# PEER gates of all 128 tokens of the first tile by indirect DMAs; norm scales by a product that also transposes

## The chip, the cores and the metric

One core of one Trainium2 chip runs the program. The metric is device time in microseconds (us), the median of several runs; lower is better. PE is TensorE, DVE VectorE, ACT ScalarE, POOL GpSimd, SP the engine that issues the ordinary DMAs.

## The reference, cut to what matters

256 tokens of width 1024 go through two blocks in float32. Block 1: a mixer (GLA and sparse attention), cross attention to 256 memory tokens, a PEER layer, a final norm. Block 2: a mixer (HGRN and Hyena), a PEER layer, a final norm. Every sublayer starts with an RMS norm.

```python
def rms_norm(x, g):
    y = x * lax.rsqrt(jnp.mean(x * x, axis=-1, keepdims=True) + EPS)
    return y * g

def peer(xb, ...):                     # 8 heads, 16 of 128 x 128 experts each
    ...
    g = jax.nn.softmax(top_s, axis=-1)           # 8 x 16 gates per token
    act = jax.nn.gelu(einsum('td,thkd->thk', xb, down[experts])) * g
    return einsum('thk,thkd->td', act, up[experts])
```

## The kernel before

**PEER, densely.** The kernel doesn't gather experts. `down` multiplies all 16384 experts with all 256 tokens, 128 experts `j` at a time, applies gelu and keeps the result in `Ha` (j below 64) and `Hb`, as [expert row i, j, token]. Most of its entries have gate 0. `up` then multiplies them, each times its gate, with the up table. Both stream 512 KB of weights per `j`: a DMA into `wf` (4 buffers), a cast to `wh` on ACT, a subtraction to `wl` on DVE, then three products per operand pair on PE (`mm3`: float32 as a high and a low part). A load is issued by SP in the order of the code and waits for a free `wf`.

**The gates** reach the 128 x 128 grid in two ways. For tokens 0 to 95 (`NS` = 96) `routing` computes addresses `at`, and `scatter` adds the gates with 128 indirect DMAs (L289, one per head and rank, one element per token) into two zeroed DRAM tensors, `gates1e` and `gates1o`, even and odd heads; each head's DMAs wait for those of the head before it in the same tensor. SP writes the zeros (`grids`, one piece behind each second load). `gates` reads them back, 4 `j` at a time, behind the waits for the scatter, and `halves` multiplies. For tokens 96 to 255, `gate` multiplies one-hot matrices on PE: per group of four tokens four float32 products (L1048), then one multiply on DVE. `_interleave` puts these groups between the pieces of `down`.

**Norms.** `norm_rows` sums squares of the two token tiles (t = 0, 1), takes the power -1/2 on POOL (`rstd`), and writes the scaled rows `xn` (L407 on DVE, L408 on ACT). `to_cols` transposes `xn` on PE, 8 chunks per tile (L424); `split` writes each chunk times the gain as a high part `xch` (L434, ACT) and a low part `xcl` (L437, DVE), which the next products need. There are five such norms (block 1's first, memory, cross attention, and one ahead of each PEER); `between` makes the final norm of block 1 and the first norm of block 2 in one, with rows `xn` too (L1442).

The last two pieces of `up` go together: all four accumulators `acc[t][n]` get both pieces before the next one starts, so that the first is complete while the others still run. Tile's scheduler sets the order on each engine, with waits by semaphores.

Of the kernel before, what the change touches and what calls it, by code (L numbers as in the profile page):

```python
# [28 lines left out]
NS = 96  # L29
# [184 lines left out]
class _Kernel:  # L214
    def __init__(self, tc, ctx, A):
# [11 lines left out]
        self.los = []  # L227
# [30 lines left out]
    def grids(self, name):  # L258


        G = [self.dr.tile([P * P * NS, 1], F32, name=name + y) for y in "eo"]
        v = [y.rearrange("(p x) o -> p (x o)", p=P) for y in G]
        n = P * NS // 12

        def blanks():
            for x in range(24):
                d = self.nc.sync.dma_start(v[x % 2][:, x // 2 * n:x // 2 * n + n].rearrange("p (a t) -> p a t", t=T),
                                           self.zero[:, None, :].to_broadcast([P, n // T, T])).ins
# [47 lines left out]
    def stream(self, src, n=1024, pool_lo=False):  # L316
# [3 lines left out]
        with self.tc.high_priority(offset=1):  # L320
# [9 lines left out]
            if not pool_lo:  # L330
                self.los.append(lo)
            if self.ahead == 3:
# [56 lines left out]
    def square(self, x, ss, dve=False):  # L389
# [4 lines left out]
        else:  # L394
            self.nc.scalar.activation(scr, x, AF.Square, accum_out=ss)

    def norm_rows(self, h, xn, urgent):

        nc = self.nc
        hv, xv = (y.rearrange("p t (a d) -> p t a d", a=2) for y in (h, xn))  # L400
# [9 lines left out]
        return xn  # L410
# [6 lines left out]
    def to_cols(self, src, dst, chunks, gain=None, c0=0):  # L417
# [26 lines left out]
    def norm_cols(self, h, gi, dst, pool, xn=None, urgent=False):  # L444
        xn = pool.tile([P, 2, D], F32, name="xn", tag="xn", bufs=1) if xn is None else xn
        self.norm_rows(h, xn, urgent)
        dst = dst or self.cols("xc")
        self.to_cols(xn, dst, range(8), lambda c: self.gains[:, gi * 8 + c:gi * 8 + c + 1])
        return dst
# [3 lines left out]
    def setup(self):  # L453
# [8 lines left out]
        self.zero = self.pc.tile([P, T], F32, name="zero")  # L462
# [107 lines left out]
    def block1_mix(self, mkT, mc, hm, pf):  # L570
        nc, A, tc = self.nc, self.A, self.tc
        with ExitStack() as st:
            pool = lambda name, bufs=1: st.enter_context(tc.tile_pool(name=name, bufs=bufs))
            p, pn = pool("b1"), pool("nsa")
            with tc.tile_pool(name="b1n", bufs=1) as px:
                x = self.norm_cols(self.h, 0, None, px)
# [4 lines left out]
            with tc.tile_pool(name="gla", bufs=1) as pg, tc.tile_pool(name="glaw", bufs=2) as pw:  # L581
                with tc.tile_pool(name="cmp", bufs=1) as pc:
# [3 lines left out]
                    self.norm_cols(hm, 2, mc, None, hm)  # L586
# [289 lines left out]
    def cross(self, mkT, mv, mem_k, mem_v):  # L876
        nc, A, tc = self.nc, self.A, self.tc
        with tc.tile_pool(name="xa", bufs=2) as pw, tc.tile_pool(name="xa1", bufs=1) as p:
            x = self.norm_cols(self.h, 1, None, pw, urgent=True)
# [46 lines left out]
    def routing(self, pool, qT, sk, split_tiles, res, keep, G):  # L926
# [4 lines left out]
        for i in range(2):  # L931
# [73 lines left out]
            if i == 0:  # L1005
# [9 lines left out]
            s = slice(i * P, i * P + P)  # L1015

            for w in range(2):
                nc.vector.tensor_copy(ji[:, 1 - w, s], b[:, w, :, None].to_broadcast([P, P, 2]))
            nc.vector.tensor_copy(gf[:, s], b[:, 2])
            yield 1  # L1020

    def gate(self, H, res, oh, at):
# [7 lines left out]
        def hot(t0):  # L1030
            ts = slice(t0, t0 + N)
# [8 lines left out]
        for t0 in range(T - N, NS - 1, -N):  # L1040
            (e, a), more = nxt, iter(hot(t0 - N)) if t0 > NS else iter((None, None))
            for t4 in (4, 0):
# [3 lines left out]
                for x in range(4):  # L1046
                    nc.scalar.mul(c[:, x], e[:, t4 + x], gf[:, t0 + t4 + x:t0 + t4 + x + 1])  # L1047
# [39 lines left out]
    def up(self, w, H, G, pool, acc, first):  # L1087
# [11 lines left out]
        for js in [(j,) for j in range(P - 2)] + [(P - 2, P - 1)]:  # L1099
# [18 lines left out]
    def peer(self, x, wq, nq, skname, dn, up, gain, G):  # L1118
        nc, A, tc = self.nc, self.A, self.tc
        with ExitStack() as st:  # L1120
# [3 lines left out]
            pa = e(tc.tile_pool(name="pact", bufs=2))  # L1124
            ha = e(tc.tile_pool(name="pha", bufs=1))
            res = [pi.tile([P, 2, T, 2], BF, name="ji"), pi.tile([P, T], F32, name="g2")]
# [14 lines left out]
            _interleave(self.down(A[dn], range(64, P - 2), x, H, pa, at), self.gate(H, res, oh, at), 0.7)  # L1141
# [278 lines left out]
    def between(self, h, acc, g, y, xn):  # L1420
# [3 lines left out]
        hv, yv, xv = (u.rearrange("p t (a d) -> p t a d", a=2) for u in (h, y, xn))  # L1424
        r1 = []
        for t in range(2):
            sh, sy = [self.small.tile([P, 2], F32, name="ss" + n, tag="ss" + n) for n in "hy"]
# [8 lines left out]
            nc.vector.tensor_scalar(sh[:, 0:1], sh[:, 0:1], 1.0 / D, EPS, op0=ALU.mult, op1=ALU.add)  # L1436
            nc.vector.tensor_scalar(sh[:, 1:2], sh[:, 0:1], EPS, None, op0=ALU.mult)
            nc.vector.scalar_tensor_tensor(out=sy[:, 0:1], in0=sy[:, 0:1], scalar=1.0 / D, in1=sh[:, 1:2],
                                           op0=ALU.mult, op1=ALU.add)
# [4 lines left out]
            r1.append(sh)  # L1444
        for t in range(2):
            nc.vector.tensor_scalar(y[:, t], y[:, t], r1[t][:, 0:1], None, op0=ALU.mult)
# [17 lines left out]
    def peer_in(self, gi):  # L1464

        self.nc.sync.dma_start(self.hsave, self.h)
        with self.tc.tile_pool(name="pxn", bufs=1) as xp:
            return self.norm_cols(self.h, gi, None, xp, urgent=True)

    def build(self):  # L1470
        tc = self.tc
        with tc.tile_pool(name="h1", bufs=1) as ph:
# [5 lines left out]
            with tc.tile_pool(name="xap", bufs=1) as p:  # L1478
# [10 lines left out]
        with tc.tile_pool(name="h2", bufs=1) as ph:  # L1489
            self.h = ph.tile([P, 2, D], F32, name="hmid")  # L1490
            with tc.tile_pool(name="b2n", bufs=1) as pn:
# [30 lines left out]
```

## Time and profile before

| | |
|---|---|
| median of 3 runs | 2338.53 us (2338.26 to 2341.12) |
| the profiled execution's own time | 2340.53 us |
| its span | 2338.7 us |
| PE busy | 2293.0 us (98%) |
| DVE, ACT, POOL busy | 72%, 52%, 20% |

The span is what the profiler sees of the execution; the own time also has what lies around it. Busy time is summed over the span; a matmul's recorded duration overlaps the next one's, so that what a product takes of PE is the distance between starts.

### The profile page before, as it was taken

The page shows a single profiled execution, that of the slowest core. Times are in us where ns is not written, and L with a number is a line of the kernel's source. Part 1 is how long each engine was busy: PE and PEld are TensorE (multiplying, and loading weights), DVE is VectorE, ACT ScalarE, POOL GpSimd, SP SyncE. Part 2 cuts the span into 40 slices and gives each one's busy share as a digit, 9 for nine tenths or more (in the row PEclk, how much of TensorE's full clock was granted, in tenths as well). Part 3 has the DMA queues.
Part 4 walks back from the last instruction along what each step waited for, and adds up shares of the span by engine and source line. Part 5 has one row for each costly group of instructions (what it writes and reads, how often), then busy time and mean ns, then how long its engine had stood idle before and what let it go on. Part 6 is the DMA issues. An engine that isn't in the chain of part 4 may idle for free.

```text
span 2338.7 us, 40753 instructions
## 1 busy us (share of the span) xinstructions
PE 2293.0 (98%) x15262; PEld 2088.2 (89%) x15262; DVE 1686.6 (72%) x3316; ACT 1220.9 (52%) x2288; POOL 470.8 (20%) x324
## 2 busy tenths in 40 slices
PE   8999999999999999999899999999999999999998
PEld 6976889999999888888899999899999999888886
DVE  6677559896666667766778886679886666666666
ACT  6555444456665444544554434445456665444444
POOL 0002010688820000000100000200888800000000
PEclk9999999999999999999899999999999999999999
DMA  7433777676655777766885444555676656667764
GB/s 238 138 115 123 233 224 217 176 185 164 153 151 170 248 228 223 223 222 212 276 256 167 153 148 150 172 180 181 163 189 155 154 151 219 223 223 225 227 223 149
DMA packets 188679, 445.86 MB, mean 191 GB/s; under 512 B 46219, under 2 KB 94528, under 8 KB 187328
## 3 DMA queue, kind: packets, MB, share of 16 engines
q1 hardware_dynamic: 159808, 443.13, 59.7%
q0 software_dynamic: 28672, 0.11, 3.2%
q8 instruction: 120, 1.97, 0.3%
q14 instruction: 79, 0.65, 0.1%
HBM read 411.61 MB, written 31.03 MB: 189 GB/s over the span
## 4 chain that ended last, share of the span: by engine, by line
PE 91%; DVE 5%; ACT 1%; issue 1%; POOL 1%; DMA 0%; POOLq 0%; SPq 0%; DVEq 0%; ACTq 0%
PE lin L350 17%; PE lin L348 17%; PE lin L349 17%; PE bank L350 11%; PE bank L348 11%; PE bank L349 10%; PE bank L1048 3%; DVE wl L329 1%; PE bank L1318 1%; PE bank L424 1%; PE bank L717 0%; PE bank L836 0%; ACT wh L322 0%; POOL y L547 0%; POOL rstd L386 0%
## 5 line engine op out<-in xcount | busy, mean ns | idle before, releaser
L329 DVE TENSOR_TENSOR wl<-wf,wh 128x1024 fp32r<-128x1024 f32 (+1 forms) x698 | 852.8, 1223 | 301.9 <-ACT wh L322 297.6
L322 ACT CAST wh<-wf 128x1024 fp32r<-128x1024 f32 x704 | 735.0, 1045 | 614.4 <-PE lin L349 447.0
L348 PE MATMUL lin<-xch,wh 128*128 128x256 f32 x2912 | 835.8, 287 | 1.3 <-ACT wh L322 1.1
L350 PE MATMUL lin<-xch,wl 128*128 128x256 f32 x2912 | 827.6, 284 | 2.3 <-DVE wl L329 1.5
L349 PE MATMUL lin<-xcl,wh 128*128 128x256 f32 x2912 | 826.5, 284 | 0.0
L350 PEld LDWEIGHTS lin<-xch,wl 128*128 128x128 f32 x2912 | 559.7, 192 | 4.4 <-DVE wl L329 3.0
L348 PEld LDWEIGHTS lin<-xch,wh 128*128 128x128 f32 x2912 | 560.7, 193 | 3.1 <-ACT wh L322 1.4
L349 PEld LDWEIGHTS lin<-xcl,wh 128*128 128x128 f32 x2912 | 560.3, 192 | 0.0
L350 PE MATMUL bank<-wh,al 128*128 128x512 f32 x1024 | 404.0, 395 | 0.0
L349 PE MATMUL bank<-wl,ah 128*128 128x512 f32 x1024 | 404.0, 395 | 0.0
L348 PE MATMUL bank<-wh,ah 128*128 128x512 f32 x1024 | 404.0, 395 | 0.0
L350 PEld LDWEIGHTS bank<-wh,al 128*128 128x128 f32 x1024 | 192.9, 188 | 45.2
L349 PEld LDWEIGHTS bank<-wl,ah 128*128 128x128 f32 x1024 | 192.9, 188 | 44.9
L348 PEld LDWEIGHTS bank<-wh,ah 128*128 128x128 f32 x1024 | 192.9, 188 | 44.8
L386 POOL TENSOR_TENSOR rstd<-rstd,mhalf 128x1 f32<-128x1 f32 (+1 forms) x18 | 13.3, 744 | 817.2 <-DVE rstd L385 752.0
L1082 ACT CAST ah<-Hb 128x256 fp32r<-128x256 f32 x128 | 52.0, 406 | 181.8 <-PE bank L349 181.8
L1082 ACT CAST ah<-Ha 128x256 fp32r<-128x256 f32 x128 | 52.0, 406 | 176.1 <-PE bank L349 173.2
L289 POOL DMA_INDIRECT gates2e<-gn,at x64 | 104.0, 1625 | 131.3 <-DVE gn L1003 112.1
L289 POOL DMA_INDIRECT gates1e<-gn,at x64 | 104.7, 1637 | 110.5 <-DMA wf<-in_p_dn_dram 91.6
L1047 ACT ACTIVATE c<-e,g 128x128 f32<-128x128 bf16 x320 | 110.9, 403 | 0.0
L1054 DVE TENSOR_TENSOR Ha<-bank,Ha 128x256 f32<-128x256 f32 x80 | 34.0, 425 | 103.3 <-PE bank L1048 102.6
L289 POOL DMA_INDIRECT gates2o<-gn,at x64 | 100.4, 1568 | 19.5 <-issue 19.5
(425 smaller groups left out, 2847.8 us busy)
## 6 DMA issues: line engine op xcount, KB each, us to landing
wf<-in_p_dn_dram SPq DMA_DIRECT2D x256, 512.0 KB
wf<-in_p_up_dram SPq DMA_DIRECT2D x256, 512.0 KB
wf<-in_w2t_dram SPq DMA_DIRECT2D x64, 512.0 KB
wf<-in_p_wq_dram SPq DMA_DIRECT2D x24, 512.0 KB
wf<-in_w_out_dram SPq DMA_DIRECT2D x16, 512.0 KB
wf<-in_w2k_dram SPq DMA_DIRECT2D x16, 512.0 KB
wf<-in_w1t_dram SPq DMA_DIRECT2D x12, 512.0 KB
gates1e<-zero SPq DMA_DIRECT2D x12, 512.0 KB
```

The lines of the kernel that those rows point to most:

```text
L289: d = self.nc.gpsimd.indirect_dma_start(y[:, :], bass.IndirectOffsetOnAxis(ap=at[:, q:q + 1], axis=0), g[0:NS, q:q + 1], None, compute_op= ...
L322: hi = self.hi = nc.scalar.copy(wh[:, :n], wf[:, :n]).ins
L329: lo = eng.tensor_tensor(out=wl[:, :n], in0=wf[:, :n], in1=wh[:, :n].bitcast(F32), op=ALU.subtract).ins
L348: mm(out, a[0], b[0], start=start, stop=False)
L349: mm(out, a[0], b[1], start=False, stop=False)
L350: self.mm = mm(out, a[1], b[0], start=False, stop=stop).ins
L424: nc.tensor.transpose(b[:, t * P:(t + 1) * P], src[:, t, (c - c0) * P:(c - c0 + 1) * P], self.ident)
L1047: nc.scalar.mul(c[:, x], e[:, t4 + x], gf[:, t0 + t4 + x:t0 + t4 + x + 1])
L1048: nc.tensor.matmul(b[:, :, x], a[:, t4 + x], c[:, x], start=True, stop=True)
L1054: nc.vector.tensor_tensor(out=hv[:, :n], in0=bv[:, :n], in1=hv[:, :n], op=ALU.mult)
L1082: self.nc.scalar.copy(ah, hj)
L1318: nc.tensor.matmul(b[:, h].rearrange("p (b w m) -> p b w m", w=2, m=m), A[:, h, i * P:i * P + P], q, start=True, stop=True)
```

## The change

`NS` becomes 128: all tokens of the first tile go by the indirect DMAs, each with 128 elements; the DRAM tensors grow from 6 to 8 MB each and are zeroed by 32 writes of 512 KB instead of 24, and the first tile's three transposes in `routing` go. `gate` has tokens 128 to 255 left: 32 groups instead of 40 in each PEER. In block 1 the zeros start early in the mixer (after three pairs of loads) instead of ahead of cross attention. `halves` and `gates` work on 128 tokens.

The norms write no `xn`. `scales` puts the scale of each token on a diagonal (128x128, DVE), and `to_cols` multiplies the unscaled rows with it, a plain float32 product in place of the transpose. In `between`, one power of two columns replaces two powers, the scaling of `hmid` moves behind the diagonals, and the first four loads' casts are ordered behind the last square and the last diagonal. The last three pieces of `up` go together instead of two.

```diff
-NS = 96
+NS = 128
...
-    def grids(self, name):
+    def grids(self, name, skip=0):
...
-        n = P * NS // 12
+        n = P * NS // 16
         def blanks():
-            for x in range(24):
+            for x in range(skip):
+                yield x
+            for x in range(32):
...
+            if self.held[0] > 0:
+                self.held[0] -= 1
+                self.after(hi, self.held[1])
+                self.after(lo, self.held[2])
...
+    def scales(self, r):
+        d = self.small.tile([P, P], F32, name="diag", tag="diag", bufs=2)
+        self.dg = self.nc.vector.tensor_scalar(d, self.ident, r, None, op0=ALU.mult).ins
+        return d
...
-        r = [self.rstd_of(ss[t]) for t in range(2)]
-        for t, k in ((0, 0), (0, 1), (1, 0)):
-            nc.vector.tensor_scalar(xv[:, t, k], hv[:, t, k], r[t], None, op0=ALU.mult)
-        nc.scalar.mul(xv[:, 1, 1], hv[:, 1, 1], r[1])
+        d = [self.scales(self.rstd_of(ss[t])) for t in range(2)]
...
-                nc.tensor.transpose(b[:, t * P:(t + 1) * P], src[:, t, (c - c0) * P:(c - c0 + 1) * P], self.ident)
+                rows = src[:, t, (c - c0) * P:(c - c0 + 1) * P]
+                if diag:
+                    nc.tensor.matmul(b[:, t * P:(t + 1) * P], rows, diag[t], start=True, stop=True)
...
                 self.scatter(G[0], at, g)
+                yield 1
+                continue
...
-        for js in [(j,) for j in range(P - 2)] + [(P - 2, P - 1)]:
+        for js in [(j,) for j in range(P - 3)] + [range(P - 3, P)]:
...
-            pa = e(tc.tile_pool(name="pact", bufs=2))
+            pa = e(tc.tile_pool(name="pact", bufs=3))
...
-            _interleave(self.down(A[dn], range(64, P - 2), x, H, pa, at), self.gate(H, res, oh, at), 0.7)
+            _interleave(self.down(A[dn], range(64, P - 2), x, H, pa, at), self.gate(H, res, oh, at), 0.56)
...
-            for q in (sy, sh):
-                nc.gpsimd.tensor_tensor(q[:, 0:1], q[:, 0:1], self.mhalf, op=ALU.pow)
-            nc.vector.tensor_scalar(xv[:, t, 0], yv[:, t, 0], sy[:, 0:1], None, op0=ALU.mult)
-            nc.scalar.mul(xv[:, t, 1], yv[:, t, 1], sy[:, 0:1])
+            nc.gpsimd.tensor_tensor(r, r, self.mhalf[:, 0:1].to_broadcast([P, 2]), op=ALU.pow)
+            d2.append(self.scales(r[:, 1:2]))
...
+        self.held = [4, self.sq, self.dg]
...
+                G = self.grids("gates1", 3)
                 self.block1_mix(mkT, mc, hm, p)
                 mv = p.tile([P, 2, D], F32, name="mv", tag="mv")
-                G = self.grids("gates1")
```

**Where instructions stand now.** DVE in the norm ahead of block 2's PEER, before (`hmid` are the rows; L414 and L385 make the scale of tile 0, then of tile 1):

```order
L568 TENSOR_TENSOR hmid<-lin,hmid 128x512 x2
L414 TENSOR_TENSOR ss<-ss 128x1
L385 TENSOR_SCALAR rstd<-ss 128x1
L407 TENSOR_SCALAR xn<-hmid,rstd 128x512 x2
L414 TENSOR_TENSOR ss<-ss 128x1
L385 TENSOR_SCALAR rstd<-ss 128x1
L407 TENSOR_SCALAR xn<-hmid,rstd 128x512
L437 SCALAR_TENSOR_TENSOR xcl<-bank,gains,xch 128x256 x8
```

And the same place in the changed kernel (line numbers are its own):

```order
L580 TENSOR_TENSOR hmid<-lin,hmid 128x512 x2
L423 TENSOR_TENSOR ss<-ss 128x1
L391 TENSOR_SCALAR rstd<-ss 128x1
L406 TENSOR_SCALAR diag<-ident,rstd 128x128
L423 TENSOR_TENSOR ss<-ss 128x1
L391 TENSOR_SCALAR rstd<-ss 128x1
L406 TENSOR_SCALAR diag<-ident,rstd 128x128
L450 SCALAR_TENSOR_TENSOR xcl<-bank,gains,xch 128x256 x8
```

A diagonal of 128 columns stands where rows of 512 stood, twice for tile 0 and once for tile 1.

ACT in `between`, before, from the last squares on (`xn` are the scaled rows, `idfth` and `wh` casts of loaded weights):

```order
L395 ACTIVATE lin,ssh<-hres 128x512
L1443 ACTIVATE xn<-hmid,ssy 128x512
L395 ACTIVATE lin,ssy<-hmid 128x512
L1443 ACTIVATE xn<-hmid,ssy 128x512
L495 CAST idfth<-wf 128x256
L434 ACTIVATE xch<-bank,gains 128x256 x6
L322 CAST wh<-wf 128x1024
L434 ACTIVATE xch<-bank,gains 128x256 x2
```

And in the changed kernel (`lbl` is a small constant of block 2's mixer):

```order
L401 ACTIVATE lin,ssh<-hres 128x512
L401 ACTIVATE lin,ssy<-hmid 128x512
L324 CAST wh<-wf 128x1024
L1238 ACT_TABLE_LOAD
L1238 ACTIVATE lbl<-lbl 128x16
L447 ACTIVATE xch<-bank,gains 128x256 x5
L324 CAST wh<-wf 128x1024
L447 ACTIVATE xch<-bank,gains 128x256 x3
```

The half rows `xn` are gone, the first cast of weights stands ahead of `xch`, and an exponential with its table load has moved in from far earlier.

PE at the end of `up` in the changed kernel, from the second of the last three pieces on:

```order
L354 MATMUL bank<-wh,ah 128x512
L355 MATMUL bank<-wl,ah 128x512
L356 MATMUL bank<-wh,al 128x512
L354 MATMUL bank<-wh,ah 128x512 x2
L355 MATMUL bank<-wl,ah 128x512
L356 MATMUL bank<-wh,al 128x512
L354 MATMUL bank<-wh,ah 128x512
L355 MATMUL bank<-wl,ah 128x512
L356 MATMUL bank<-wh,al 128x512
L355 MATMUL bank<-wl,ah 128x512
L356 MATMUL bank<-wh,al 128x512
```

The last piece's `wh` product for the first accumulator is followed by six products of the second accumulator with the two pieces before it, and only then by those that need its `wl` and its `al`. The first accumulator is complete after 15 of 36 products (6 of 24 before), the second after 18 (12 of 24).

## Rows read from the trace of the kernel before

**Rows 1.** The page: span, busy, GB/s in slices, chain by engine, two costly groups.
```profile
span 2338.7 us, 40753 instructions
...
PE 2293.0 (98%) x15262; PEld 2088.2 (89%) x15262; DVE 1686.6 (72%) x3316; ACT 1220.9 (52%) x2288; POOL 470.8 (20%) x324
...
GB/s 238 138 115 123 233 224 217 176 185 164 153 151 170 248 228 223 223 222 212 276 256 167 153 148 150 172 180 181 163 189 155 154 151 219 223 223 225 227 223 149
...
PE 91%; DVE 5%; ACT 1%; issue 1%; POOL 1%; DMA 0%; POOLq 0%; SPq 0%; DVEq 0%; ACTq 0%
...
L329 DVE TENSOR_TENSOR wl<-wf,wh 128x1024 fp32r<-128x1024 f32 (+1 forms) x698 | 852.8, 1223 | 301.9 <-ACT wh L322 297.6
L322 ACT CAST wh<-wf 128x1024 fp32r<-128x1024 f32 x704 | 735.0, 1045 | 614.4 <-PE lin L349 447.0
```

**Rows 2.** Waits of PE: line, releaser, us in total, times, longest.
```profile
PE bank L424 <- DVE xn L407: 14.4, 6, 8.2
PE bank L424 <- DVE xn L1442: 5.3, 2, 4.2
```

**Rows 3.** Windows: length, busy by engine, granted clock, DMA share, GB/s.
```profile
526.00:762.00 236.00, 236.00 (x1993) 236.00 (x1992) 154.01 (x264) 150.45 (x402) 115.33 (x75) 1.00 0.60 159
...
1120.00:1130.00 10.00, 4.10 (x16) 2.69 (x15) 8.45 (x26) 7.09 (x19) 3.05 (x4) 0.63 0.65 193
1130.00:1140.00 10.00, 8.65 (x52) 7.97 (x52) 7.41 (x11) 5.82 (x9) 0.00 (x0) 0.69 1.03 372
```

**Rows 4.** Instructions by line: ns min/median/max, first and last start in us.
```profile
L1048 PE MATMUL bank<-c,a x640: 271/275/275, 549.1 to 1956.0; 128*128 128x128 f32 x160
...
L348 PE MATMUL lin<-xch,wh x1248: 277/283/582, 21.1 to 762.7; 128*128 128x256 f32 x179
...
L289 POOL DMA_INDIRECT gates1e<-gn,at x64: 1415/1416/2475, 420.6 to 634.3; - x64
L289 POOL DMA_INDIRECT gates1o<-gn,at x64: 1415/1416/2336, 453.0 to 662.5; - x64
```

**Rows 5.** The chain in order of time: start, us; two gate groups.
```profile
549.24 0.89 PE bank L1048 x8
553.00 0.89 PE bank L1048 x8
```

**Rows 6.** Timeline of SP at block 1's first read of gates.
```profile
738.38 0.33 SPq L302 DMA_DIRECT2D gt<-gates1e  x1
...
741.53 3.43 SPq L250 DMA_DIRECT2D wf<-in_p_dn_dram  x2
```

**Rows 7.** Timeline of the norm ahead of block 2's PEER.
```profile
1508.83 0.88 DVE L407 TENSOR_SCALAR xn<-hmid,rstd 128x512 f32<-128x512 f32 x2 [0.67 <-POOL rstd L386]
1509.46 1.06 PE L424 MATMUL bank<-ident,xn 128*128 128x128 f32 x8 [2.29 <-DVE xn L407]
1509.63 0.15 DVE L414 TENSOR_TENSOR ss<-ss 128x1 f32<-128x1 f32 x1
...
1511.19 0.67 PE L424 MATMUL bank<-ident,xn 128*128 128x128 f32 x4 [0.66 <-DVE xn L407]
```

**Rows 8.** Timeline of `between`, PE and one row of ACT.
```profile
1119.57 0.39 PE L349 MATMUL bank<-wl,ah 128*128 128x512 f32 x1
1119.80 0.40 PE L350 MATMUL bank<-wh,al 128*128 128x512 f32 x1
1124.38 1.97 PE L424 MATMUL bank<-ident,xn 128*128 128x128 f32 x8 [4.18 <-DVE xn L1442]
1127.43 1.12 PE L424 MATMUL bank<-ident,xn 128*128 128x128 f32 x4 [1.08 <-DVE xn L1442]
1131.54 0.58 PE L348 MATMUL lin<-xch,wh 128*128 128x256 f32 x1 [1.10 <-ACT wh L322]
...
1137.25 0.57 ACT L1371 ACTIVATE hx<-lin,cw 128x256 f32<-128x256 f32 x1 [2.10 <-PE lin L350]
```

**Rows 9.** Timeline of ACT: a table load.
```profile
0.72 1.28 ACT L395 ACT_TABLE_LOAD   x1 [0.72 <-PEq L1510]
```

More of the change, by code (lines that the diff above doesn't have):

```diff
@@ L423, in to_cols @@
                 b = banks[n // 2][:, n % 2]
-                nc.tensor.transpose(b[:, t * P:(t + 1) * P], src[:, t, (c - c0) * P:(c - c0 + 1) * P], self.ident)
+                rows = src[:, t, (c - c0) * P:(c - c0 + 1) * P]
+                if diag:
+                    nc.tensor.matmul(b[:, t * P:(t + 1) * P], rows, diag[t], start=True, stop=True)
+                else:
+                    nc.tensor.transpose(b[:, t * P:(t + 1) * P], rows, self.ident)
                 if t == 1:
@@ L442, in cols, with norm_cols @@
         return (p.tile([P, 8, T], F32R, name=tag + "h", tag=tag + "h"), p.tile([P, 8, T], F32R, name=tag + "l", tag=tag + "l"))
-    def norm_cols(self, h, gi, dst, pool, xn=None, urgent=False):
-        xn = pool.tile([P, 2, D], F32, name="xn", tag="xn", bufs=1) if xn is None else xn
-        self.norm_rows(h, xn, urgent)
+    def norm_cols(self, h, gi, dst, urgent=False):
+        diag = self.norm_rows(h, urgent)
         dst = dst or self.cols("xc")
-        self.to_cols(xn, dst, range(8), lambda c: self.gains[:, gi * 8 + c:gi * 8 + c + 1])
+        self.to_cols(h, dst, range(8), lambda c: self.gains[:, gi * 8 + c:gi * 8 + c + 1], diag=diag)
         return dst
@@ L461, in setup @@
         self.tcol = self.const("tcol", [P, 1])
-        self.zero = self.pc.tile([P, T], F32, name="zero")
+        self.zero = self.pc.tile([P, P], F32, name="zero")
         nc.gpsimd.memset(self.zero, 0.0)
@@ L574, in block1_mix @@
             p, pn = pool("b1"), pool("nsa")
-            with tc.tile_pool(name="b1n", bufs=1) as px:
-                x = self.norm_cols(self.h, 0, None, px)
+            x = self.norm_cols(self.h, 0, None)
             h2 = self.filter_net(pf)
@@ L1014, in routing @@
                 nc.tensor.transpose(b[:, w], (*ij, g)[w], self.ident)
-            s = slice(i * P, i * P + P)
             for w in range(2):
-                nc.vector.tensor_copy(ji[:, 1 - w, s], b[:, w, :, None].to_broadcast([P, P, 2]))
-            nc.vector.tensor_copy(gf[:, s], b[:, 2])
+                nc.vector.tensor_copy(ji[:, 1 - w], b[:, w, :, None].to_broadcast([P, P, 2]))
+            nc.vector.tensor_copy(gf, b[:, 2])
             yield 1
@@ L1030, in hot @@
         def hot(t0):
-            ts = slice(t0, t0 + N)
+            ts = slice(t0 - P, t0 - P + N)
             e, a = [oh.tile([P, N, P], d, name=n) for n, d in (("e", BF), ("a", F32))]
@@ L1123, in peer @@
             oh = e(tc.tile_pool(name="poh", bufs=2))
-            pa = e(tc.tile_pool(name="pact", bufs=2))
+            pa = e(tc.tile_pool(name="pact", bufs=3))
             ha = e(tc.tile_pool(name="pha", bufs=1))
-            res = [pi.tile([P, 2, T, 2], BF, name="ji"), pi.tile([P, T], F32, name="g2")]
+            res = [pi.tile([P, 2, P, 2], BF, name="ji"), pi.tile([P, P], F32, name="g2")]
             H = [ha.tile([P, 64, T], F32, name="Ha")]
@@ L1418, in hyena, with between @@
             yield
-    def between(self, h, acc, g, y, xn):
+    def between(self, h, acc, g, y):
         nc = self.nc
-        hv, yv, xv = (u.rearrange("p t (a d) -> p t a d", a=2) for u in (h, y, xn))
-        r1 = []
+        hv, yv = (u.rearrange("p t (a d) -> p t a d", a=2) for u in (h, y))
+        r1, d2 = [], []
         for t in range(2):
-            sh, sy = [self.small.tile([P, 2], F32, name="ss" + n, tag="ss" + n) for n in "hy"]
+            sh, sy, r = [self.small.tile([P, 2], F32, name="ss" + n, tag="ss" + n) for n in "hyr"]
             for k in range(2):
@@ L1466, in peer_in @@
         self.nc.sync.dma_start(self.hsave, self.h)
-        with self.tc.tile_pool(name="pxn", bufs=1) as xp:
-            return self.norm_cols(self.h, gi, None, xp, urgent=True)
+        return self.norm_cols(self.h, gi, None, urgent=True)
     def build(self):
@@ L1490, in build @@
             self.h = ph.tile([P, 2, D], F32, name="hmid")
-            with tc.tile_pool(name="b2n", bufs=1) as pn:
-                xn = pn.tile([P, 2, D], F32, name="xn")
-                self.between(h, acc, g, self.h, xn)
-                x = self.cols("xc")
-                self.to_cols(xn, x, range(8), lambda c: self.gains[:, 32 + c:33 + c])
+            r, d = self.between(h, acc, g, self.h)
+            x = self.cols("xc")
+            self.to_cols(self.h, x, range(8), lambda c: self.gains[:, 32 + c:33 + c], diag=d)
+            for t in range(2):
+                self.after(self.nc.vector.tensor_scalar(self.h[:, t], self.h[:, t], r[t][:, 0:1], None, op0=ALU.mult).ins, self.dg)
             G = self.grids("gates2")
```

33 lines of the change are left out of this document (16 added, 17 removed).

## The prediction, made before the changed kernel ran

> **What bounds the kernel now.** I read the page first, then the chain, the waits of PE, and windows of the stages that the change touches. PE is busy for 2293.0 of 2338.7 us and has 91% of the chain that ended last [rows 1]; it is idle for 45.7 us in all. In the stretch of `down` into which the gate groups are put, PE is busy for 236.0 of 236.0 us at granted clock 1.00, while DVE, ACT and POOL are busy for 154, 150 and 115 [rows 3]. A product that leaves PE there therefore shortens the end by its whole length, until something else becomes the bound. Outside, PE waits most visibly at the norms: 14.4 us in six waits for `xn` of L407, 5.3 us in two for `xn` of L1442 [rows 2]. Behind `between` it also runs slowly: the granted clock is 0.63 and 0.69 in the two windows after it [rows 3], that is, part of the time at 1.2 GHz instead of 2.4, after PE had been idle for 4.18 us and then waited again for 1.08 and 1.10 us [rows 8].
>
> **Gate groups, removed.** A group of four tokens is 8 rows of PE (640 rows for 320 tokens, [rows 4]) and has 0.89 us on the chain [rows 5]; 71 such rows stand there, all alike. Each PEER loses 8 of 40 groups: 16 x 0.89 = 14.2 us. The first tile's transposes in `routing` go too, 3 in each PEER. In the norm ahead of block 2's PEER eight transposes take 1.06 us [rows 7], 0.13 each, so this is 6 x 0.13 = 0.8 us. What was hidden, the copies on ACT and the multiplies on DVE of those groups, brings nothing. Together **-15.0**.
>
> **Indirect DMAs, larger.** Their number stays at 128 in each PEER, with 128 elements instead of 96. One takes 1.415 us at the least and up to 2.475; the first starts at 420.6, the last at 662.5 [rows 4], so 127 steps of 1.905 us. No row shows one of 128 elements. Lower bound: a fixed cost, 1.905 again. Upper bound: all of it grows by 128/96, 2.54 us. I take the middle of a growth of the shortest duration alone (0 to 0.47): 2.14, which ends 127 x 0.24 = 30 us later, at about 694. The first read of gates is issued at 738.38 [rows 6], some 8 us sooner in the changed kernel, at 730. So there is cover for 36 us, and the cost is **0**. Without the cover: SP issues in order, and behind the two reads of gates stand the last two loads of `p_dn` and then those of `p_up`, so that a late scatter starves PE.
>
> By the Trainium skill, SBUF — State Buffer, section SBUF: two separate sides, DVE and GpSimd share a port pair under an exclusive lock, and GpSimd's building of descriptors stops for it. By that rule the excess over the shortest time, 1.605 us in the mean without the gap of 0.30, is waiting that doesn't grow with the elements, and the upper bound falls from 2.54 to 1.905 + 0.47 = 2.38; the trace has the excess, but doesn't show its cause.
>
> **Zeros and reads.** 8 more writes of 512 KB in each PEER. The most that the DMA moved in a window is 372 GB/s [rows 3]; the first slice of 58.5 us, which now gets about six of these writes (3.1 MB), moves 238 GB/s [rows 1], so (372 - 238) x 58.5 = 7.8 MB are free there. Cost 0; if all of it stood in the way, 3.1 MB / 372 GB/s = 8.5 us. Later slices have 150 to 230 GB/s. The reads grow by a third of 384 KB in each four pieces of `up`, where the slices have 223 GB/s: 0.
>
> **Norms.** For each, two things change. First, tile 1 no longer stands behind tile 0's rows on DVE. In [rows 7] the two `xn` take 0.88 us, and L414 of tile 1 starts at 1509.63. The diagonal has 128 columns; DVE needs 0.15 us for one column and 0.44 for 512, so about 0.23. L414 then starts at about 1509.0, and tile 1's diagonal is ready at 1510.3. Second, PE's work grows. A float32 product of this shape is two rows of L1048, 0.89 / 4 = 0.223 us at full clock, against 0.13 for a transpose [rows 5, 7]. Tile 0's eight products start at 1509.1 and end at 1510.9, only then tile 1's can start: 0.3 us sooner than 1511.19. With PE less idle I also expect a little less time at half clock. I take -0.5 for each of the two norms ahead of a PEER, **-1.0**; bounds -2.0 each (no fall of the clock) and +1.4 each (the eight products at half clock end 1.8 us later). The other three norms (first, memory, attention) have work of other kinds beside them; 48 products x 0.09 = 4.3 us, half of it hidden in waits: **+2.0** (0 to +4.3).
>
> **`between`.** PE's last product of `up` starts at 1119.80, the first of the next mixer at 1131.54, and that one's first tile of results reaches ACT at 1137.25 [rows 8]: 17.4 us. In the changed kernel the accumulators are complete sooner: 21 and 18 products before the end instead of 18 and 12, at 0.23 us each (1119.80 - 1119.57) 0.7 and 1.4 us. Tile 1's scale loses three things ahead of it: half a row `xn` on ACT, the scaling of `hmid` on DVE, and one of two powers on POOL. I place tile 1's first product 1 us sooner, and the first weights are cast before the columns `xch` instead of behind six of them. Against that stand the products at half clock (eight in 3.5 us; transposes took 1.97 [rows 8]) and, on ACT ahead of `xch`, a table load of 1.28 us [rows 9] with an exponential that waits for a load issued late. I get the first tile some 13.5 us after the last product, and take **-3.5**; bounds -6.0 (full clock throughout) and +1.0 (the exponential late by 2 us, half clock). At the end of the program the earlier accumulators help DVE alone: **-0.4** (0 to -1.1).
>
> The last three pieces need all three buffers of `wl`. The last `wl` can only be made when the piece before the three is done, and takes a cast of 1.05 and a subtraction of 1.22 us [rows 1]. The order has 13 products, 3.0 us, ahead of the one that needs it: **0**.
>
> **Sum.** -15.0 - 3.5 - 1.0 + 2.0 - 0.4 = -17.9. The profiled execution's own time was 2340.5 us, 2.0 above the median of the runs; 2340.5 - 17.9 - 2.0 = **2320.6 us** for the median.
>
> **The rivals.**
>
> *The scatter is late.* All of the time per DMA grows by a third or more. Reads would be due 310 us after the start (738.4 - 8 - 420.6), and the loads behind them may be some 9.5 us late: 741.53 for a load whose products run from about 757, six pieces later, since the last product of `down` starts at 762.7 [rows 4, 6] and a piece takes 553.00 - 549.24 - 0.89 = 2.87 [rows 5]; landing and splitting need some 6. At 2.54 us a DMA the end is 325 us after the start, PE loses 5.5 us in each PEER, and the time is 2332. For: the elements are a third more, and nothing in the rows separates a fixed part. Against: 36 us of cover at my price. It decides over faster or slower at 2.58 us: then 330 us, 10.5 us lost twice, 2341; above that the change is a loss.
>
> *Half clock at the norms.* Four norms start PE from idle (the first, two ahead of a PEER, `between`). If their eight products run at half clock, each is 8 x 0.223 = 1.8 us later, and the gains there (4.5) are lost: 2320.6 + 7.1 + 4.5 = 2332. For: the clock behind `between`. Against: PE starts sooner and works more densely than with the transposes.
>
> *Products four times as dear as transposes.* 96 products in six norms at 4 x 0.13 each, 0.39 x 96 = 37.4 us more on PE, of which two thirds would not be hidden: 2320.6 + 24.9 - 2 = 2343, slower. The Trainium skill, TensorE: Matmul & The Clock Gate, section Terms, gives transposes of float32 as four times faster. The rows of L1048, plain float32 products of the same shape, say 0.223 / 0.13 = 1.7.
>
> *Loads late in block 1* behind the early zeros: half of the 8.5 us, 2325.
>
> *The groups cost nothing now*, since what ran beside them fills PE's place: `down` would wait for casts. Then only the norms count: 2335. Against: ACT and DVE are busy for 64% there.
>
> **How the numbers follow.** Chances: the forecast 0.70; half clock 0.12; late scatter 0.08, half of it beyond the point that decides; late loads 0.05; groups for nothing 0.03; dear products 0.02. The forecast's own range is 2313 to 2328. The range that leaves out no more than two in ten has to reach toward the cases at 2332: 2311 to 2330. About 0.2% (4.7 us) is what a measurement of this kernel can tell from no change: faster 0.88, same 0.06, slower 0.06.
>
> **What would show it.** Right: 512 rows of gate products instead of 640, and PE still fully busy around them; the last indirect DMA ending before 725 and the reads of gates issued without a wait near 730; in the norms a product row pair each 0.22 us, tile 1's within 1.8 us of tile 0's; from the last product of `up` to the first tile of results 13 to 15 us. Wrong: SP waiting for POOL at the first read; granted clock under 0.9 behind the norms ahead of the PEERs; PE waiting for `wl` in the last three pieces; ACT waiting for `wf` in the first 60 us.

## The result, and the profile after

The changed kernel takes 2316.73 us (median of 4 runs, 2312.25 to 2319.11) against 2338.43 for the kernel before beside it: the medians are 21.7 us apart. The ratio on record, 0.9894 with a 95% interval of 0.9883 to 0.9906, would be 24.8 us, so an amount that is read from two ratios below is good to some 3 or 4 us. The forecast was 2320.6, the range 2311 to 2330. The sum was right within 4 us, but not for the reasons given: two amounts that no term had, about +7 us in block 1 and 11 to 14 us less in `up`, are in it.

The page of the changed kernel, profiled execution (own time 2319.11 us): span, busy, chain by engine and by line.

```profile
span 2317.3 us, 40583 instructions
...
PE 2272.2 (98%) x15224; PEld 2083.2 (90%) x15224; DVE 1653.8 (71%) x3257; ACT 1195.0 (52%) x2201; POOL 518.5 (22%) x322
...
PE 79%; DVE 10%; DMA 5%; issue 2%; ACT 2%; POOL 1%; SPq 0%; DVEq 0%; POOLq 0%; ACTq 0%
PE lin L356 16%; PE lin L354 16%; PE lin L355 16%; PE bank L355 8%; PE bank L354 7%; PE bank L356 7%; DVE wl L331 4%; DMA gt<-gates1o 3%; PE bank L1060 2%; PE bank L1330 1%; DMA gt<-gates2o 1%; ACT wh L324 1%; PE bank L435 1%; DVE al L1096 0%; DVE cand L979 0%
```

PE is busy for 20.8 us less than in [rows 1] and idle for 45.1 us as before. New in the chain are the reads of gates (`DMA gt<-gates1o`, 3%) with DVE behind them.

Where the 21.4 us of span come from is seen by stretches. Each ends where a named instruction starts on its engine's timeline; `after_0` is an experiment below.

| stretch up to | before, us | after, us | difference | forecast | after_0 minus before |
|---|---|---|---|---|---|
| first `mem_v` product | 263.1 | 272.3 | +9.2 | +2.0 (three norms) | +6.8 |
| first indirect DMA | 157.5 | 157.6 | 0.0 | -0.5 (norm) | -1.1 |
| first product of `up`, block 1 | 342.5 | 334.6 | -7.9 | -7.5 (gate groups) | -7.9 |
| first spectrum product of block 2 | 442.5 | 433.1 | -9.4 | -3.5 (`between`) | -4.6 |
| block 2's first indirect DMA | 425.5 | 427.4 | +1.9 | -0.5 (norm) | +2.1 |
| first product of `up`, block 2 | 342.3 | 334.5 | -7.8 | -7.5 (gate groups) | -7.8 |
| end of the span | 365.4 | 357.9 | -7.5 | -0.4 | 0.0 |

**Gates.** Instructions of the gate products, of the indirect DMAs (ns min/median/max, first and last start in us), and SP's first read, in the changed kernel:

```profile
L1060 PE MATMUL bank<-c,a x512: 272/275/276, 557.5 to 1942.1; 128*128 128x128 f32 x171
...
L291 POOL DMA_INDIRECT gates1e<-gn,at x64: 1546/1566/2583, 429.9 to 665.0; - x64
L291 POOL DMA_INDIRECT gates1o<-gn,at x64: 1547/1555/2765, 466.7 to 697.7; - x64
...
739.83 0.33 SPq L304 DMA_DIRECT2D gt<-gates1e  x1
```

512 product rows are left of 640. A DMA of 128 elements takes at least 1.546 us against 1.415 [rows 4]; 127 steps from 429.9 to 697.7 are 2.11 us each, 42 us ahead of the first read.

**Norm and `between`.** Timeline of the norm ahead of block 2's PEER, then of `between`, changed kernel:

```profile
1502.84 0.29 DVE L406 TENSOR_SCALAR diag<-ident,rstd 128x128 f32<-128x128 f32 x1 [0.67 <-POOL rstd L392]
1503.27 2.92 PE L435 MATMUL bank<-diag,hmid 128*128 128x128 f32 x24 [2.13 <-DVE ss L423]
1504.06 0.29 DVE L406 TENSOR_SCALAR diag<-ident,rstd 128x128 f32<-128x128 f32 x1 [0.68 <-POOL rstd L392]
1506.08 0.51 PE L354 MATMUL lin<-xch,wh 128*128 128x256 f32 x2
...
1115.85 0.39 PE L356 MATMUL bank<-wh,al 128*128 128x512 f32 x1
1118.00 2.02 PE L435 MATMUL bank<-diag,hmid 128*128 128x128 f32 x16 [1.76 <-issue]
1120.93 1.16 PE L435 MATMUL bank<-diag,hmid 128*128 128x128 f32 x8 [0.91 <-DVE diag L406]
1122.19 0.39 PE L354 MATMUL lin<-xch,wh 128*128 128x256 f32 x1
1130.05 0.56 ACT L1383 ACTIVATE hx<-lin,cw 128x256 f32<-128x256 f32 x1
```

Each float32 product is two rows: 24 of the 32 are done in 2.92 us, without a gap between tile 0 and tile 1. In `between` the first tile of results comes 14.2 us after the last product of `up` instead of 17.4 [rows 8].

**Block 1.** Windows, first of before, then of the changed kernel, from 100 us to the first `mem_v` product and three pieces of it (length, busy by engine, granted clock, DMA share, GB/s):

```profile
100.00:263.10 163.10, 156.08 (x1007) 130.47 (x1003) 113.11 (x238) 88.38 (x205) 22.74 (x24) 0.98 0.48 156
...
100.00:130.00 30.00, 29.49 (x217) 27.81 (x214) 19.48 (x49) 15.68 (x36) 2.26 (x3) 0.89 0.31 102
130.00:150.00 20.00, 19.98 (x136) 16.34 (x135) 16.92 (x44) 12.11 (x26) 0.84 (x2) 1.00 0.58 198
185.00:215.00 30.00, 28.68 (x163) 21.11 (x162) 19.94 (x44) 15.10 (x38) 3.70 (x5) 1.00 0.31 102
```

```profile
100.00:272.30 172.30, 162.65 (x1032) 137.64 (x1031) 109.06 (x234) 87.09 (x202) 21.19 (x23) 0.94 0.55 169
...
100.00:130.00 30.00, 29.46 (x207) 28.16 (x206) 17.37 (x38) 13.66 (x26) 2.03 (x2) 0.83 0.53 163
130.00:150.00 20.00, 20.00 (x146) 18.34 (x146) 16.48 (x46) 13.53 (x32) 0.31 (x1) 1.00 0.76 222
185.00:215.00 30.00, 24.15 (x120) 17.29 (x121) 19.38 (x49) 14.19 (x43) 5.54 (x6) 0.84 0.24 71
```

The 9.2 us lost are 2.6 more of idle PE (9.65 against 7.02) and 6.6 more of busy PE, for hardly more instructions. The second part is the clock: (1 - granted clock) times length gives 3.3 us before, all ahead of 130, and 5.1 + 4.8 = 9.9 after.

**`up`.** Windows of both `up` stages, first before, then changed:

```profile
850.00:1050.00 200.00, 200.00 (x862) 162.18 (x861) 139.60 (x240) 98.69 (x145) 0.00 (x0) 1.00 0.71 225
2050.00:2250.00 200.00, 200.00 (x862) 162.16 (x861) 138.64 (x234) 97.00 (x144) 0.00 (x0) 1.00 0.70 225
```

```profile
850.00:1050.00 200.00, 199.84 (x880) 164.53 (x879) 139.61 (x237) 99.39 (x147) 0.00 (x0) 1.00 0.71 238
2050.00:2250.00 200.00, 199.82 (x879) 164.40 (x878) 139.20 (x241) 99.52 (x147) 0.00 (x0) 1.00 0.70 240
```

PE had no wait before, and yet does 880 products now where it did 862, at the same clock. The distance between starts fell from 200 / 862 = 0.232 to 0.227 us. Single rows show it too: three products take 0.69 to 0.71 us before, 0.68 after (899.11 to 899.79):

```profile
899.03 0.40 PE L348 MATMUL bank<-wh,ah 128*128 128x512 f32 x1
899.27 0.40 PE L349 MATMUL bank<-wl,ah 128*128 128x512 f32 x1
899.51 0.40 PE L350 MATMUL bank<-wh,al 128*128 128x512 f32 x1
899.74 0.39 PE L348 MATMUL bank<-wh,ah 128*128 128x512 f32 x1
```

```profile
899.11 0.39 PE L354 MATMUL bank<-wh,ah 128*128 128x512 f32 x1
899.33 0.39 PE L355 MATMUL bank<-wl,ah 128*128 128x512 f32 x1
899.56 0.39 PE L356 MATMUL bank<-wh,al 128*128 128x512 f32 x1
899.79 0.39 PE L354 MATMUL bank<-wh,ah 128*128 128x512 f32 x1
```

So two things had no term: block 1's clock, and closer products in `up`.

### The profile page after: what moved, and what is told of

Same layout as the page of the kernel before. It is cut to its first block, busy times and chain, and to the rows that moved or that the text cites. A ratio compares the mean times of both kernels' runs of the same rounds, so it can differ in the third digit from the quotient of the medians.

```text
span 2317.3 us, 40583 instructions
## 1 busy us (share of the span) xinstructions
PE 2272.2 (98%) x15224; PEld 2083.2 (90%) x15224; DVE 1653.8 (71%) x3257; ACT 1195.0 (52%) x2201; POOL 518.5 (22%) x322
## 4 chain that ended last, share of the span: by engine, by line
PE 79%; DVE 10%; DMA 5%; issue 2%; ACT 2%; POOL 1%; SPq 0%; DVEq 0%; POOLq 0%; ACTq 0%
PE lin L356 16%; PE lin L354 16%; PE lin L355 16%; PE bank L355 8%; PE bank L354 7%; PE bank L356 7%; DVE wl L331 4%; DMA gt<-gates1o 3%; PE bank L1060 2%; PE bank L1330 1%; DMA gt<-gates2o 1%; ACT wh L324 1%; PE bank L435 1%; DVE al L1096 0%; DVE cand L979 0%
## 5 line engine op out<-in xcount | busy, mean ns | idle before, releaser
L356 PE MATMUL bank<-wh,al 128*128 128x512 f32 x1024 | 398.9, 390 | 0.0
L354 PE MATMUL bank<-wh,ah 128*128 128x512 f32 x1024 | 398.8, 390 | 0.0
L291 POOL DMA_INDIRECT gates2e<-gn,at x64 | 117.3, 1833 | 132.2 <-PE lin L356 113.0
L291 POOL DMA_INDIRECT gates1e<-gn,at x64 | 117.3, 1833 | 110.6 <-DMA wf<-in_p_dn_dram 91.4
L291 POOL DMA_INDIRECT gates1o<-gn,at x64 | 113.4, 1771 | 19.5 <-issue 19.5
L291 POOL DMA_INDIRECT gates2o<-gn,at x64 | 113.3, 1770 | 19.5 <-issue 19.5
L310 DVE TENSOR_TENSOR gt<-gt 128x512 f32<-128x512 f32 x64 | 44.2, 691 | 100.6 <-DMA gt<-gates2o 51.5
```

The source lines that it names most:

```text
L291: d = self.nc.gpsimd.indirect_dma_start(y[:, :], bass.IndirectOffsetOnAxis(ap=at[:, q:q + 1], axis=0), g[0:NS, q:q + 1], None, compute_op= ...
L310: self.nc.vector.tensor_tensor(out=g[:, 0], in0=g[:, 0], in1=g[:, 1], op=ALU.add)
L354: mm(out, a[0], b[0], start=start, stop=False)
L356: self.mm = mm(out, a[1], b[0], start=False, stop=stop).ins
```

## The experiments

All times are medians; ratios are to the kernel before on the same chip in the same rounds, with 95% intervals.

**1. Early zeros alone.** In the kernel before:

```diff
+                G = self.grids("gates1", 3)      # skip as in the change, still 24 writes
                 self.block1_mix(mkT, mc, hm, p)
-                G = self.grids("gates1")
```

> The kernel before with one part of the change alone: the 24 zero writes of gates1 start at the weight loads of block 1 (three skipped) and not at those of the attention. Block 1 of the changed kernel reached the first mem_v product 9.2 us later than before (272.3 against 263.1). If the early zeros cause that, by the DMA engines or by the order that they give to the program, this kernel is some 9 us slower, about 2347 us, with the first mem_v product at about 272. If the products with the norm's scales cause it, it stays at 2338.5 within 1 us and at 263.

2342.7 us, ratio 1.001 (1.0001 to 1.0019): some 2 us, which is neither of the two. The first `mem_v` product is at 268.1, with half clock near 125, 140 and 210 us; PE's idle time is that of before.

**2. Three norms back to scaled rows.** In the changed kernel:

```diff
-                    self.norm_cols(hm, 2, mc)
+                    self.norm_cols(hm, 2, mc, xn=hm)     # likewise the first and the attention's norm
```

> The changed kernel with the first, the memory's and the attention's norm back at scaled rows and transposes; the two PEER norms, the step between the blocks, the zeros and the gates stay as changed. If these three norms cost block 1 its 9 us, the first mem_v product is back at about 263 and the time falls to about 2307.5 us. If the early zeros do, it stays at 272 and the time at 2315 to 2317.

2320.5 us, 0.9905 (0.9887 to 0.9924): not told apart from the changed kernel. The first `mem_v` product comes at 266.3, 6.0 us sooner, but both `up` stages run slower (0.2347 and 0.2334 us a product), because reads of gates land late. What block 1 gained was lost there.

**3 and 4. The third activation buffer.**

```diff
-            pa = e(tc.tile_pool(name="pact", bufs=3))
+            pa = e(tc.tile_pool(name="pact", bufs=2))
```

> The changed kernel with two buffers instead of three for the activation halves in PEER. In the changed kernel the products of the up stage follow each other every 0.2265 us, before every 0.2315, some 7 us in each of the two stages. If the third buffer gives that, the spacing is 0.2315 again and the time about 2331 us. If it comes from elsewhere (the gate tile of 512 columns, where tiles lie in SBUF), the spacing stays and the time is 2317 within 2 us.

> The kernel before with the third buffer for the activation halves alone. If the buffer shortens the spacing of the up products, 0.2265 us and about 2324 us; if not, 0.2315 us and 2338.5 within 1 us.

Without it the changed kernel takes 2326.6 us, 0.9944 (0.9927 to 0.996); with it alone the kernel before takes 2339.1, 0.999 (0.9981 to 0.9999). The buffer doesn't bring the closer products: with two, `up` of block 1 runs at 0.2262, that of block 2 at 0.2315, where the weight loads now wait 5.8 us for `al`. It covers late gate reads, which the kernel before hardly has (DVE waits 3.1 us for them in 770 to 1100 us).

**5. The gates alone** in the kernel before (`NS = 128`, with `routing`, `gate`, 32 zeros started ten pairs of loads into the mixer):

> The kernel before with the gates' part alone: 128 tokens by indirect DMAs, 32 groups left in each PEER, 32 zero writes that start eight writes ahead of where the 24 started; norms, the step between the blocks and the activation buffers as before. The groups and the routing's transposes are worth 15 us: if that is all, about 2323.5 us with up products every 0.2315 us. If the gates also bring the closer products of the up stage (0.2265 us, some 7 us in each PEER), it comes to 2309 to 2313, or up to 2320 where gate reads land late and stall TensorE.

2327.9 us, 0.9948 (0.9933 to 0.9964). Both `down` stages gain (up to the first product of `up` 335.1 and 334.8 us), `up` stays at 0.232: the groups and no more. By the medians it is 12.8 us faster than the kernel before, where 15 were expected.

**6. A wider gate tile alone** in the kernel before:

```diff
-        g = pool.tile([P, 2, 4, NS], F32, name="gt", bufs=2)
+        g = pool.tile([P, 2, 4 * 128], F32, name="gt", bufs=2)[:, :, :4 * NS].rearrange(...)
```

> The kernel before with its gate tile allocated as wide as in the changed kernel, 512 columns a half instead of 384, of which it uses 384: only where the tiles of PEER lie in SBUF moves. If that place gives the closer products, they follow every 0.2265 us and the time is about 2324 us. If the shape of the gate reads or of the work gives them, the spacing is 0.2315 us and the time 2338.5 within 1.5 us.

2341.7 us, 1.0002 (0.9993 to 1.0011), spacing 0.232. It moves `al` by 2 KB: no effect. That ruled out this displacement, not every one.

**7. The gates' sum later.** In the changed kernel:

```diff
-                gt.append(self.gates(G, j + 4, pool))
+                new.append(self.gates(G, j + 4, pool))        # reads only
...
+            if j % 4 == 2 and new:
+                gt.append(self.both(new.pop(), self.los[-1]))  # the sum, behind this piece's wl
```

> The changed kernel with the sum of the two gate reads placed four weight splits later on VectorE behind its reads. VectorE waited 47.7 us for these reads in 770 to 1100 us of the changed kernel. If these waits reach TensorE through late weight splits, they vanish, the up products follow every 0.2262 us without stalls and the time falls by 2 to 4 us to about 2314 us; if they are covered, it stays at 2317.

2314.3 us, 0.9891 (0.9872 to 0.9910): in time not told apart from the changed kernel. The waits of 770 to 1100 us, first of the changed kernel, then of this one:

```profile
DVE gt L310 <- DMA gt<-gates1o: 47.7, 22, 3.7
...
PEld bank L355 <- DVE wl L331: 3.9, 7, 1.2
PE bank L355 <- DVE wl L331: 1.4, 4, 0.8
```

```profile
ACT ah L1100 <- PE bank L361: 87.1, 64, 1.4
ACT ah L1100 <- issue: 77.4, 57, 1.4
DVE wl L337 <- ACT wh L330: 48.3, 92, 0.5
DVE al L1102 <- ACT ah L1100: 45.2, 92, 0.7
```

DVE's waits for the reads are gone and with them those of PE; both stages run at 0.2262 without a stall. In the profiled executions that is worth 429.3 against 433.1 us in the row of the table with block 1's `up`, and 356.7 against 357.9 in the last.

**8. A combination:** the changed kernel with the norms of 2, the zeros started seven writes later, and the reads of gates two pieces earlier with the sum later; the multiplications by the gates move too, four pieces at once right behind each sum.

> The changed kernel with the scaled rows and transposes back in the first, the memory's and the attention's norm, the zero writes started seven writes later in block 1, and the gate reads issued two pieces earlier with their sum later. If block 1's loss comes from these norms and from the early zeros, and the late gate reads stall the up stage, the three give 6, 2 and 2 to 4 us: about 2306 us, with the first mem_v product at about 264. If the losses are chance of the order, 2317.

2309.7 us, 0.9869 (0.9852 to 0.9887), the fastest of all; its interval overlaps that of the changed kernel (from 0.9883 on), so how much faster is not settled. The first `mem_v` product is at 263.9, both `up` stages at 0.2262.

**9 to 12. The place of the stationary halves.** What separates the kernels at 0.2262 from those at 0.232 is where tiles start in each partition of SBUF, in the programs as built. The moving weights `wh` and `wl` start 128 bytes past a multiple of 512 in both kernels. The stationary `ah`, `al`, `mch`, `mcl`, `ych` and `ycl` start at a multiple of 512 before and 128 past one after. All size changes are multiples of 512 bytes but one: the small tile `r` in `between`, 4 buffers of 32 bytes.

```diff
# before_128 (kernel before); gates_128 is the kernel of 5 with the same line
+        self.small.tile([P, 32], F32, name="pad", bufs=1)
# before_zero: that line, and ahead of all other tiles
+        self.pc.tile([P, 96], F32, name="padc")
# after_0 (changed kernel)
-            sh, sy, r = [self.small.tile([P, 2], F32, name="ss" + n, tag="ss" + n) for n in "hyr"]
+            sh, sy = [self.small.tile([P, 4], F32, name="ss" + n, tag="ss" + n) for n in "hy"]
+            r = sh[:, 2:4]
```

> The kernel before with an unused tile of 128 bytes a partition ahead of the tiles of the stages, so that the stationary halves (ah and al of up, mch and mcl, ych and ycl) lie at the same place within 512 bytes as the moving weights, as they do in the changed kernel. Nothing else moves. If that place gives the closer products of 512 columns, they follow every 0.2265 us instead of 0.2315 to 0.2325 us, and the time falls by 12 to 14 us to about 2326 us. If the changed kernel got them from anything else, it stays at 2338.5 within 1.5 us.

> The kernel before with stationary halves and moving weights both at a multiple of 512 bytes (they lay at 0 and at 128 past one; the changed kernel has both at 128). If what counts is that the two are alike, the products follow every 0.2265 us and the time is about 2326 us. If what counts is where the stationary halves lie by themselves (128 good, 0 bad), the spacing is 0.2315 us and the time 2338.5 within 1.5 us.

> The kernel before with the gates' part alone (2327.9 us in an earlier run) and the unused tile of 128 bytes. If the place gives the closer products, it gains 8 to 13 us more, less where late gate reads stall the up stage: 2315 to 2320 us, as fast as the whole change within 4 us, so that the norm part is worth nothing in sum. If not, 2328.

> The changed kernel with the two columns of the exponents' result kept in the tile of the row sums, which takes a small tile of 128 bytes away and puts the stationary halves back at a multiple of 512 bytes, the moving weights staying 128 past one. If the place gives the closer products, they are 0.2315 us apart again and the time goes up by 8 to 13 us to 2325 to 2330 us. If not, it stays at 2316.7 within 3 us.

| kernel | stationary, moving (bytes past 512) | `up` spacing, us | time, us | ratio |
|---|---|---|---|---|
| before_128 | 128, 128 | 0.2262, 0.2262 | 2324.8 | 0.9927 (0.9913 to 0.9940) |
| before_zero | 0, 0 | 0.2262, 0.2265 | 2323.7 | 0.9923 (0.9909 to 0.9937) |
| gates_128 | 128, 128 | 0.2320, 0.2304 | 2322.2 | 0.9921 (0.9907 to 0.9935) |
| after_0 | 0, 128 | 0.2317, 0.2317 | 2328.8 | 0.9952 (0.9940 to 0.9964) |

The windows of block 1's `up` in before_128, before_zero and after_0, one fence each:

```profile
850.00:1050.00 200.00, 200.00 (x884) 165.62 (x883) 141.58 (x243) 101.25 (x150) 0.00 (x0) 1.00 0.69 230
```

```profile
850.00:1050.00 200.00, 200.00 (x884) 165.62 (x883) 141.40 (x243) 101.32 (x150) 0.00 (x0) 1.00 0.69 231
```

```profile
850.00:1050.00 200.00, 200.00 (x863) 162.14 (x862) 141.22 (x234) 97.78 (x144) 0.00 (x0) 1.00 0.70 235
```

The unused 128 bytes give 17 us to the kernel before (15 by the medians), and taking 128 bytes away costs the changed kernel 0.9952 - 0.9894, or 13.6 us (10.6 by the medians, each beside its own kernel before). It is not the place of the stationary tile alone: at 0 and 0 the products are as close as at 128 and 128. The unused tile moves all tiles of the stages by 128 bytes, not the halves alone; but the pace is read where PE waits for nothing, and weights and halves are what these products read. gates_128 missed its forecast of 2315 to 2320 by 2 us. It has closer products too, but stalls: in 850 to 1050 us DVE waits 38.7 us for gate reads and PE and its weight loads 8.4 for `al`, with two activation buffers.

before_128 has the instruction order of the kernel before on every engine, and still its first `mem_v` product comes 5.7 us later in the profiled execution. Its windows in block 1:

```profile
100.00:268.75 168.75, 162.13 (x1010) 136.43 (x1011) 113.87 (x238) 88.61 (x205) 23.24 (x25) 0.94 0.46 151
...
100.00:130.00 30.00, 29.49 (x192) 27.67 (x193) 17.60 (x42) 12.98 (x26) 2.72 (x4) 0.77 0.26 95
130.00:150.00 20.00, 20.00 (x134) 18.59 (x134) 15.26 (x44) 13.44 (x31) 0.31 (x1) 0.83 0.50 165
```

PE is idle for 6.6 us (before 7.0), and the clock costs 6.9 + 3.4 = 10.3: what the changed kernel loses to it, without any of its norms, zeros or reordering. This is one execution, and executions of one program differ by as much: those of before_128 have spans from 2318.1 us at a mean granted clock of 0.995 to 2324.3 at 0.991, those of the kernel before beside it from 2336.1 at 0.994 to 2345.0 at 0.991.

## Why the prediction came out right, and where it was wrong

**Gate groups and transposes (-15.0): right.** -7.9 and -7.8 are -15.7.

**Indirect DMAs (0): right.** The step was put at 2.14 us between 1.905 and 2.54 and is 2.11, with an end at 698 instead of 694. The shortest DMA grew by 0.131 us for 32 elements, so most of its time is fixed (an even growth would make 96 x 0.131 / 32 = 0.39 of the 1.415 us, an estimate). The rival of a late scatter fell: SP issued the reads at 739.83 without waiting for POOL (not near 730, since block 1 came to `down` 9 us later). The Trainium skill, SBUF — State Buffer, section SBUF: two separate sides, has GpSimd locked out of the port pair that it shares with DVE, and unable to write descriptors, while DVE runs certain operations. If the excess over the shortest time were waiting for that lock, it would not grow, and a step would be an estimated 1.905 + 0.131 = 2.04 us. Measured are 0.07 more; the mean excess without the gap went from 0.19 to 0.26 us (two rows of 117.3 and 113.4 us for 128 DMAs are 1.80 each). No run shows the cause of the excess.

**Zeros (0): right within 2 us**, by the experiment that starts them early. The loads of the first 60 us weren't held up. **Reads of gates (0): wrong in the mechanism, small in the sum.** I saw room in the slices' GB/s and did not ask when a read lands. Reads a third larger behind loads that come sooner land after DVE wants them. Alone neither does it (in 770 to 1100 us 8.8 us of waits in after_0, 5.8 in before_128, no stall of PE); together they make 47.7 us of waits, and 3.8 and 1.2 us of span. The third buffer, to which I gave no price, is what keeps it that small: without it the changed kernel loses 11.7 us by the ratios, 7.6 by the medians.

**Norms ahead of the PEERs (-1.0): too hopeful by 1 at least.** From the last product ahead of block 2's norm to the first product behind it 5.33 us, before 5.29: the diagonal is ready sooner, as worked out (0.29 us for 0.23), but 16 rows of products stand where 8 transposes stood, and the two cancel. No half clock came at this norm in the changed kernel's profiled execution. It did in that of after_0, where 6.91 us pass instead of 5.33, and in that of experiment 3, where it is 6.38; after_0:

```profile
1500.00:1510.00 10.00, 7.90 (x48) 7.11 (x47) 4.54 (x15) 4.47 (x12) 2.86 (x3) 0.83 0.56 183
```

So the rival "half clock at the norms" is not refuted: in those two executions it made this norm 1.1 and 1.6 us longer.

**Other three norms (+2.0): of the right size or too low; not settled.** In the kernels with diagonals in these norms (the changed one and experiments 3, 7 and 12) PE is idle for 7.9 to 9.6 us between 90 us and the first `mem_v` product, in the others for 5.2 to 7.1, the means 2.2 apart. But in the changed kernel PE waits there for `diag` for 0.6 us only, and taking these norms back (experiment 2) brought the first `mem_v` product 6.0 us sooner. Products four times as dear as transposes would have cost 24.9. Between starts, a product's two rows take 0.223 us in the norm ahead of block 2's PEER, and a transpose took 0.109 there before; the 0.13 of the forecast has the end of the last of eight in it [rows 7]. The Trainium skill's factor of four (TensorE: Matmul & The Clock Gate, section Terms) doesn't hold here: the trace says 2.0.

**The step that failed in block 1** is "Half clock at the norms": I looked for it only behind norms that start PE from idle, and counted none in block 1. There the clock cost 10.2 us from 100 us to the first `mem_v` product, before 3.4 (summed over windows of 2 us), each in the one execution that was profiled. This is no property of the change that I can name: kernels with early zeros alone (10.2), with the gates alone (10.2) and with an unused tile and the old order (10.2) have it, the wide gate tile has 1.7. That so different kernels share it is shown; whether the program or the chance of an execution makes it is not, nor which wait sets it off. Over the whole span (1 - granted clock) times length is 18.6 us before and 19.3 after: what block 1 lost to the clock, the stretches behind it got back.

**`between` (-3.5): right in its size**, -4.6 in after_0, where `up` has its old pace. The first tile of results came after 14.2 us (13.5 forecast). The clock came out better than forecast: tile 0's eight products were put at half clock and 3.5 us, and their 16 rows took 2.02 at full clock. The two windows behind the last product of `up`, changed kernel, have a granted clock of 0.93 and 0.90 where [rows 3] has 0.63 and 0.69:

```profile
1115.00:1125.00 10.00, 6.41 (x39) 5.33 (x38) 8.86 (x29) 8.81 (x21) 1.44 (x2) 0.93 1.01 302
1125.00:1135.00 10.00, 10.00 (x77) 9.99 (x77) 8.20 (x14) 5.93 (x10) 0.00 (x0) 0.90 0.80 244
```

From the last product of `up` to the first spectrum product, after_0 takes 4.8 us less than the kernel before: half clock while PE was busy cost 1.7 us instead of 4.4, PE is idle for 4.5 less, and its products take 2.4 more. That cost of half clock is 3.3 to 5.0 us in all eight profiled kernels with the old step and 0 to 2.2 in the six with the new one.

**End of the program (-0.4):** 0.0 to -0.2, within its bounds. In the last three pieces PE waits for nothing; its 1.4 us of waits for `wl` in `up` lie earlier, behind the late reads.

**The step that is missing** is the pace of `up`, which I took as fixed: 0.23 us a product. It is 0.2262 when the stationary halves start as far past 512 bytes as the moving weights. 1536 products in a stage times 0.0058 are 8.9 us, which before_128 shows (356.6 us from the first product to the end, before 365.4). The changed kernel has it by the 128 bytes of a tile in `between`. Without them it stands at 0.9952, 2327.2 us beside 2338.4: -11.2, where the prediction has -17.9. Block 1's clock, +6.8 in the profiled execution, would explain the difference, but that the rest then meets the forecast to 0.1 us is luck: the interval is 2.8 us wide to either side, and single terms were off by up to 2.6 us, in both directions. That the changed kernel came within 4 us of the forecast is luck as well: a loss and a larger gain that no term had stand against each other.

Mixer 2 with its norm lost 1.9 us (2.1 in after_0), where -0.5 was forecast. Most of it is half clock, at two places: in the changed kernel's profiled execution 1.7 us at 1479 us, ahead of the norm, in after_0 the 1.6 us at the norm itself. It is -0.7 with the gates alone, where no half clock stands in this stretch. What sets it off stays open.

## What to carry to other kernels

When a stage's time changes without a wait that changed, divide its length by its instructions first: a pace of 0.232 against 0.226 us is invisible in busy shares, and here was worth about half of the gain. Before crediting an edit with it, look at where the edit moved tiles, and try an unused tile of that size alone. And one profiled execution is not enough for the price of a stretch at half clock: the executions of one kernel here differ by up to 9 us in span. Price a larger transfer by when it lands against when it is wanted, not by the bandwidth that is free.

## What the runs showed of the hardware, unexpected

- A product of 512 columns of the float32 halves (type fp32r), with a new stationary operand each time, has one of two paces in all 14 kernels: 0.2262 us where stationary and moving tiles start equally far past a multiple of 512 bytes in their partitions (0 and 0, 128 and 128), 0.2315 to 0.233 where not (0 and 128 in `ah`, `mch` and `ych`; `xcat` at 32 or 160 with weights at 0 or 128 stays at 0.233 in every kernel). Products of 256 columns in `down` keep their pace. Why, and which part of 512 counts, wasn't tried.
- The same instructions in the same order lost 3.4 us to the 1.2 GHz level in one profiled execution and 10.2 in another, of the program with tiles moved by 128 bytes, up to the same product. Executions of a single program differ in the same way (kernel before: 2336.1 us at a mean granted clock of 0.994, 2345.0 at 0.991), so the move is not shown to be the cause.
- An indirect DMA that adds single elements takes 1.415 us for 96 and 1.546 us for 128 at the least.
